# Experts taken in a mixed order of their rank, and one S5 table step issued a unit later

## Chip, core and metric

The kernel runs on one core of a Trainium2 chip, in one launch. The metric is the device time of a run in microseconds (us); lower is better. Its engines have these names here: PE (matrix products), DVE (vector), ACT (scalar and activation), POOL (GpSimd), SP (only issues transfers in this kernel). Each engine works through its own queue in order and waits for others by semaphores.

## What is computed

A two-layer trunk over 256 tokens of width 1024, all in float32. The two places that the change touches are the S5 layer and the expert layer behind it; in front of them stand an attention layer and a dense feed-forward layer (FFN). Cut to what matters:

```python
# S5: 64 groups of 16 channels, each with a 64-dim complex state
y = Re(C x_t),  x_t = a x_{t-1} + B u_t          # a, B, C are complex tables
# experts: top 2 of 8, width 2816
logits = h @ w_router
gates = softmax over the two largest logits, 0 elsewhere     # (256, 8)
for e in range(8):
    out = out + gates[:, e:e+1] * ((silu(h @ w_gate[e]) * (h @ w_up[e])) @ w_down[e])
```

The sum over the experts may be taken in any order. Each expert has 3 x 1024 x 2816 weights, about 34.6 MB, and all eight are read once.

## The kernel before

**Experts.** `route` computes the router's result on the chip, counts the tokens of each expert, and ranks the experts by that count (`rank`, 1 for the largest). A *place* is a position in the order in which the program works through experts. Which expert stands at a place is only known on the chip: `M` is the 8 x 8 matrix that is one where an expert's rank fits a place, and `self.ci` holds the expert's number of each place, from which SP takes the address of its weights (`unit`). What is fixed when the program is built is the capacity of a place, in blocks of 32 tokens: `CAPS = (4, 3, 3, 3, 3, 2, 2, 2)`. A branch (`overflow`) would serve tokens beyond the capacities.

An expert's weights come in 66 *units* of 512 KB (128 rows x 1024 float32): for each of its three column stages 16, 16 and 12 units of gate and up (`gate_up`; the third kind has the name `rest`, line 1698 and 1701, with pieces 128 wide in place of 256), and 8, 8 and 6 units of `w_down` (`down`, line 1729). For every unit PE does four products per block of 32 tokens, so a unit costs PE an amount in proportion to the capacity, and the transfers the same whatever the capacity. The down products of a stage stand behind the gate and up products of the next stage, those of the third stage behind the first stage of the next expert.

The units land in 36 buffers of 512 KB: 4 + 15 named `raw`, 6 `rawh`, 6 `rawi`, 4 `hT_hi`/`hT_lo` and 1 `rawa`. SP issues the next unit as soon as PE has released a buffer, in the order of the program. So PE can be served from a store of some units ahead. No unit can be fetched before `route` has the expert numbers.

Between the units stand, for the next expert, its gather (`gather`, line 1599), and for the present one the transposes of its selection (`back`, line 1619, once per expert and always at the same place among its `rest` units) and for the one before the scatter (line 1657). They are put there by a list that counts units (`run_queue`).

**S5 tables.** While the FFN runs, `s5_tables` builds the tables `G`, `H`, `L`, `E` of the next layer. It is a written-out schedule: `on(u, fn)` records a step at unit u of the FFN, a unit being one tile of FFN weights on PE, and `tick` runs the steps recorded for a unit after its products. For each quarter q of the table, with t0 = 14 + 10 q: `gc(q)` on POOL (24 operations, at t0 - 5), `expand` on ACT and DVE at t0 and t0 + 3 (it copies `gc`'s result to `s5x`), transposes of it on PE (line 1160) one unit after each, and on POOL the chain `hc(q, 0..3)`, 6 operations each (line 1040), whose result is copied to `H` on ACT by `hc_out(q, 0..3)` (lines 1146 and 1147).

`hc(q, t)` reads the result of `hc(q, t - 1)` and writes one of two halves of a buffer, `HC[:, t % 2]`. `hc(q, t)` is recorded at unit t0 + t and `hc_out(q, t)` at t0 + 3 + t; steps of one unit run in the order of their recording. So `hc(q, 2)` is recorded ahead of `hc_out(q, 0)`, which reads the same half: the copy waits for `hc(q, 2)`, and `hc` waits for no copy of its own quarter. Behind `hc(q, 3)` POOL does `gc(q + 1)`, and behind the last quarter the doubling of `E` (`e_double`) and then the norm's small operations (line 393 to 403) that the FFN's end waits for.

ACT and DVE also split each FFN weight tile into two parts ahead of PE (`hl`, lines 206 and 213), in the same queues as the table's copies.

Of the kernel before, what the change touches and what calls it, by code (L numbers as in the profile page):

```python
# [13 lines left out]
OP = mybir.AluOpType  # L14
# [13 lines left out]
C_M1 = C_SEL + 4  # L28
C_LOW = C_M1 + 4
C_CAP = C_LOW + 64  # L30
N_CONST = C_CAP + 8

CAPS = (4, 3, 3, 3, 3, 2, 2, 2)


def make_consts():
    c = np.zeros((128, N_CONST), np.float32)
    p = np.arange(128)
    c[:, C_ID:C_ID + 128] = np.eye(128)
    c[:, C_ONE:C_ONE + 128] = 1.0  # L40
    c[:, C_CAUS:C_CAUS + 128] = np.where(p[None, :] <= p[:, None], 0.0, NEG)
    c[:, C_TRI:C_TRI + 128] = (p[:, None] < p[None, :])
    c[:, C_IOTA:C_IOTA + 128] = p[None, :] + 1
    s = (p % 32)[:, None]
    t = np.arange(32)[None, :]
    for i, l in enumerate(LEVELS):
        if l == 0:
            m = s == t
        else:
            m = (s // (2 * l) == t // (2 * l)) & (s % (2 * l) < l) & (t % (2 * l) >= l)  # L50
        c[:, C_LVL + 32 * i:C_LVL + 32 * i + 32] = m
    for hp in range(4):
        for base in (0, 32):
            c[base + 2 * hp, C_SEL + hp] = 1.0
            c[64 + base + 2 * hp + 1, C_SEL + hp] = 1.0
    m1 = ((p // 32) % 2 == 0)
    c[:, C_M1] = m1
    c[:, C_M1 + 1] = ~m1
    c[:, C_M1 + 2] = -1.0 * ~m1
    c[:, C_CAP:C_CAP + 8] = 32.0 * np.array(CAPS)  # L60
    c[:, C_LOW:C_LOW + 64] = np.tril(np.ones((8, 8)), -1).reshape(64)
    return c

# [187 lines left out]
class Trunk:  # L251
# [10 lines left out]
    def on(self, u, fn):  # L262

        assert u > self.u
        self.sched.setdefault(u, []).append(fn)
# [770 lines left out]
    def s5_tables(self, u0):  # L1036
# [3 lines left out]
        tt = lambda o, x, y, op, e=v: e.tensor_tensor(out=o, in0=x, in1=y, op=op)  # L1040
        ts = lambda o, i, s1, s2, p, q, e=v: e.tensor_scalar(out=o, in0=i, scalar1=s1, scalar2=s2, op0=p, op1=q)
        on = lambda u, fn: self.on(u0 + u, fn)
# [69 lines left out]
        def cmul(o_r, o_i, x_r, x_i, y_r, y_i, tmp):  # L1112

            tt(o_r, x_r, y_r, OP.mult, g)
            tt(tmp, x_i, y_i, OP.mult, g)
            tt(o_r, o_r, tmp, OP.subtract, g)
            tt(o_i, x_r, y_i, OP.mult, g)
            tt(tmp, x_i, y_r, OP.mult, g)
            tt(o_i, o_i, tmp, OP.add, g)
# [3 lines left out]
        def gc(q):  # L1123

            sl = slice(8 * q, 8 * q + 8)
            GC = st["GC"] = kp.tile([128, 2, 8, 4, 16], F32, name="s5gc", tag="gate", bufs=1)
            cmul(GC[:, 0, :, 3], GC[:, 1, :, 3], bc[:, 0, sl], bc[:, 1, sl], cb(fr, sl), cb(fi, sl), tile_t())
            for t in (2, 1, 0):
                cmul(GC[:, 0, :, t], GC[:, 1, :, t], GC[:, 0, :, t + 1], GC[:, 1, :, t + 1], cb(ar, sl), cb(ai, sl),
                     tile_t())  # L1130

        def hc(q, t):

            sl = slice(8 * q, 8 * q + 8)
            if t == 0:
                st["x"] = bc[:, 2, sl], bc[:, 3, sl]
            o_r, o_i = st["HC"][:, t % 2, 0], st["HC"][:, t % 2, 1]
            cmul(o_r, o_i, *st["x"], cb(ar, sl), cb(ai, sl), tile_t())
            st["x"] = o_r, o_i
# [9 lines left out]
        def expand(u):  # L1149
            for i in range(2):  # L1150
                for h in range(2):
                    P = slice(64 * h, 64 * h + 64)
                    (v.tensor_copy if h else a.copy)(
                        st["X"][P, i].rearrange("p r t h k -> p (r t) h k")[:, :, h, :],
                        st["GC"][P, i, 4 * u:4 * u + 4].rearrange("p r t k -> p (r t) k"))

        def g_T(i):
            p = st["gT"] = self.ps([128, 4, 128])
            for r in range(4):
                nc.tensor.transpose(p[:, r, :], st["X"][:, i, r].rearrange("p t h k -> p (t h k)"), self.ident)  # L1160

        def g_out(q, u, i):
            r0 = 8 * q + 4 * u
            (v.tensor_copy if i else a.copy)(self.G[:, r0:r0 + 4, i, :], st["gT"])
# [89 lines left out]
        for q in range(4):  # L1254
            t0 = T0 + PER * q
            if q:
                on(t0 - 5, lambda q=q: gc(q))
            on(t0, lambda: expand(0))
            on(t0 + 1, lambda: g_T(0))
            on(t0 + 2, lambda q=q: (g_out(q, 0, 0), g_T(1), lag(q, 0)))  # L1260
            on(t0 + 3, lambda q=q: (g_out(q, 0, 1), lag_out(), expand(1)))
            on(t0 + 4, lambda q=q: (lag_T(0), g_T(0)))
            on(t0 + 5, lambda q=q: (g_out(q, 1, 0), g_T(1), lag(q, 1)))
            on(t0 + 6, lambda q=q: (g_out(q, 1, 1), lag_out()))
            on(t0 + 7, lambda: lag_T(1))
            on(t0 + 8, lambda q=q: l_out(q))
            for t in range(4):
                on(t0 + t, lambda q=q, t=t: hc(q, t))
                on(t0 + 3 + t, lambda q=q, t=t: hc_out(q, t))
        t0 = T0 + PER * 4 - 1  # L1270
        on(t0, e_begin)
# [183 lines left out]
    def route(self):  # L1455
        nc, kp, ex = self.nc, self.keep, self.ex
        v, a, g = nc.vector, nc.scalar, nc.gpsimd
        tt = lambda o, x, y, op, e=v: e.tensor_tensor(out=o, in0=x, in1=y, op=op)
# [23 lines left out]
        c = kp.tile([128, 2, 8, 16], F32, name="rcmp", tag="t2k", bufs=4)  # L1482
        r = ex.tile([128, 2, 8, 1], F32, name="rrank")
# [7 lines left out]
        r = r.rearrange("p t e o -> p t (e o)")  # L1491
# [19 lines left out]
        c = kp.tile([128, 8, 16], F32, name="rcmp", tag="t2k", bufs=4)  # L1511
# [4 lines left out]
        rank = ex.tile([128, 8], F32, name="rk")  # L1516
        v.tensor_reduce(out=rank, in_=c, axis=AX.X, op=OP.add)
        v.tensor_scalar(out=rank, in0=rank, scalar1=1.0, scalar2=None, op0=OP.add)
        iota = self.cst[:, C_IOTA:C_IOTA + 8]
        mt = kp.tile([128, 5, 8, 8], F32, name="rmt", tag="t2k", bufs=4)  # L1520
        M = ex.tile([128, 8, 8], F32, name="rM")
        tt(M, rank.unsqueeze(1).to_broadcast([128, 8, 8]), iota.unsqueeze(2).to_broadcast([128, 8, 8]), OP.is_equal)
        tt(mt[:, 0], M, iota.unsqueeze(1).to_broadcast([128, 8, 8]), OP.mult)
        pl = ex.tile([128, 8], F32, name="rpl")
        v.tensor_reduce(out=pl, in_=mt[:, 0], axis=AX.X, op=OP.add)
# [66 lines left out]
    def gather(self, e, part):  # L1592

        n = 32 * CAPS[e]
        p = self.gat[part] = self.ps([128, 4, 128])[:, :, :n]
# [6 lines left out]
    def gather_out(self, e, part):  # L1602
# [3 lines left out]
        for j in range(4):  # L1606
            k = 4 * part + j
            o = self.xT[e][:, k, :32 * CAPS[e]]
            if e == 0 and j % 2:
# [28 lines left out]
    def rows_hi(self, e, x):  # L1638

        n = 32 * CAPS[e]  # L1640
        h = self.keep.tile([128, 512], F32R, name="yh", tag="t2k", bufs=4)[:n]
# [3 lines left out]
    def rows_lo(self, e, x):  # L1645
        n = 32 * CAPS[e]
        l = self.keep.tile([128, 512], F32R, name="yl", tag="t2k", bufs=4)[:n]
# [4 lines left out]
    def scatter(self, e, i, p=None):  # L1652
# [3 lines left out]
        for n, y in enumerate(self.yp[x]):  # L1656
            self.nc.tensor.matmul(p, self.B[e][:32 * CAPS[e], t, :], y, start=(n == 0), stop=(n == 1))

# [404 lines left out]
    def setup(self):  # L2063
        nc, I, kp = self.nc, self.ins, self.keep
        self.cst = kp.tile([128, N_CONST], F32, name="cst")
        nc.scalar.dma_start(out=self.cst[:, C_C:C_C + 8], in_=I["consts"][:, C_C:C_C + 8])
# [134 lines left out]
```

## Time and profile before

| | us |
|---|---|
| median of 3 runs | 1375.65 |
| lowest, highest run | 1372.13, 1376.98 |
| the profiled execution's own time | 1371.33 |
| its span, first to last instruction | 1369.6 |
| PE busy | 1234.4 (90% of the span) |
| PE weight loads busy | 991.2 (72%) |
| DVE, ACT, POOL busy | 622.3, 364.7, 269.3 |

The span is divided as the program is: to about 180 us the attention projections, then attention and output projection, the FFN with the S5 tables from about 200 to 456 us, S5 to about 600 us, and from 612 us the experts, more than half of the span. The profiled execution took 1.73 us more than its span. Busy shares are means over stages with different limits.

### The profile page before, as it was taken

The numbers are of one execution on the slowest core, as the hardware profiler recorded it, in microseconds if no ns is written. First come the engines' busy times: TensorE is split into PE (matmuls) and PEld (weight loads), VectorE is DVE, ScalarE is ACT, GpSimd is POOL, SyncE is SP. The second block draws the span as 40 slices with busy tenths as digits, with TensorE's granted clock in tenths as the row PEclk, the third lists the DMA queues.
The fourth block names the chain that finished last, engine by engine and source line by source line (L and its number), as shares of the span: only waits on it lengthen the run. The fifth ranks groups of instructions, "written<-read, shape, count | busy, mean of one in ns | idle before, by whom it ended". The sixth has DMA issues, their size and how long they took to land. (4 is left out here: it accounts for less than half of the span.)

```text
span 1369.6 us, 42688 instructions
## 1 busy us (share of the span) xinstructions
PE 1234.4 (90%) x18635; PEld 991.2 (72%) x18635; DVE 622.3 (45%) x1074; ACT 364.7 (27%) x808; POOL 269.3 (20%) x324
## 2 busy tenths in 40 slices
PE   4998988689997698989989999999999999999885
PEld 4976877679886697886676779976589875756353
DVE  6999898678878686652000310310311202121113
ACT  4455444354553465720000010110010010101001
POOL 1000036999949353000000000000000000000000
PEclk9999999799999898899999999999999999999997
DMA  9867648587887221319999999989989999999994
GB/s 346 273 225 231 213 136 266 168 263 248 271 266 230 77 64 62 109 35 408 407 407 327 380 332 369 406 302 390 400 290 405 386 327 407 407 407 406 408 402 186
DMA packets 138722, 398.57 MB, mean 291 GB/s; under 512 B 12288, under 2 KB 45312, under 8 KB 138400
## 3 DMA queue, kind: packets, MB, share of 16 engines
q1 hardware_dynamic: 138176, 394.62, 79.0%
q8 instruction: 148, 2.42, 0.7%
q0 software_dynamic: 208, 1.15, 0.3%
q14 instruction: 46, 0.38, 0.1%
q10 hardware_dynamic: 144, 0.00, 0.0%
HBM read 394.67 MB, written 1.05 MB: 289 GB/s over the span
## 5 line engine op out<-in xcount | busy, mean ns | idle before, releaser
L1712 DVE TENSOR_TENSOR eh<-gu,eh 128x256 f32<-128x256 f32 (+1 forms) x66 | 25.1, 381 | 433.6 <-ACT eh L1711 433.4
L288 PE MATMUL ps<-hT_hi,hl 128*128 128x256 f32 x576 | 173.4, 301 | 13.6 <-DVE hT_hi L441 5.5
L213 DVE TENSOR_TENSOR hl<-raw,hl 128x1024 fp32r<-128x1024 f32 x121 | 159.2, 1321 | 54.3 <-ACT hl L206 54.0
L1689 PE MATMUL gu<-raw,xTs 128*32 128x256 f32 x3032 | 173.0, 379 | 2.7 <-DMA raw<-in_o_exp_up_dram 1.7
L290 PE MATMUL ps<-hT_hi,hl 128*128 128x256 f32 x576 | 170.2, 295 | 4.6 <-DVE hl L213 4.6
L289 PE MATMUL ps<-hT_lo,hl 128*128 128x256 f32 x576 | 170.4, 296 | 3.0 <-DVE hT_lo L848 2.5
L393 POOL TENSOR_TENSOR ss<-ss 128x1 f32<-128x1 f32 x10 | 2.8, 276 | 845.2 <-ACT ps L386 764.5
L206 ACT ACTIVATE hl<-raw 128x1024 fp32r<-128x1024 f32 x121 | 126.8, 1058 | 156.0 <-DMA raw<-in_e_ffn_up_dram 37.5
L1689 PEld LDWEIGHTS gu<-raw,xTs 128*32 128x32 f32 x3032 | 118.9, 110 | 51.4 <-DMA raw<-in_o_exp_up_dram 6.2
L288 PEld LDWEIGHTS ps<-hT_hi,hl 128*128 128x128 f32 x576 | 117.2, 204 | 16.7 <-DVE hT_hi L441 5.9
L1729 PE MATMUL dn<-raw,eh 128*32 128x256 f32 x2032 | 121.1, 380 | 3.1 <-DMA raw<-in_o_exp_down_dram 1.7
L290 PEld LDWEIGHTS ps<-hT_hi,hl 128*128 128x128 f32 x576 | 116.8, 203 | 6.2 <-DVE hl L213 6.2
L289 PEld LDWEIGHTS ps<-hT_lo,hl 128*128 128x128 f32 x576 | 117.1, 203 | 5.0 <-DVE hT_lo L848 3.4
L1711 ACT ACTIVATE eh<-gu 128x256 f32<-128x256 f32 (+1 forms) x66 | 22.9, 348 | 336.4 <-PE gu L1689 301.0
L1729 PEld LDWEIGHTS dn<-raw,eh 128*32 128x32 f32 x2032 | 77.1, 110 | 40.2 <-DMA raw<-in_o_exp_down_dram 6.1
L1722 DVE STREAM_TRANSPOSE eh<-eh 128x256 f32<-128x256 f32 (+1 forms) x66 | 27.1, 420 | 96.5 <-PE dn L1729 95.8
L1613 ACT ACTIVATE xTs<-ps,colo_mod_ffn,colo_mod_ffn 128x96 f32<-128x96 f32 (+2 forms) x60 | 20.8, 422 | 164.9 <-PE ps L1599 163.9
L1689 PE MATMUL gu<-rawh,xTs 128*32 128x256 f32 x992 | 58.0, 379 | 0.6 <-DMA rawh<-in_o_exp_up_dram 0.6
L1698 PE MATMUL gu<-raw,xTs 128*32 128x128 f32 x1664 | 50.2, 273 | 5.1 <-issue 4.8
L1698 PEld LDWEIGHTS gu<-raw,xTs 128*32 128x32 f32 x1664 | 45.3, 110 | 7.9 <-issue 5.6
L1689 PEld LDWEIGHTS gu<-rawh,xTs 128*32 128x32 f32 x992 | 37.3, 110 | 18.3 <-DMA rawh<-in_o_exp_up_dram 2.1
L1689 PE MATMUL gu<-rawi,xTs 128*32 128x256 f32 x848 | 49.4, 379 | 0.0
(418 smaller groups left out, 2182.5 us busy)
## 6 DMA issues: line engine op xcount, KB each, us to landing
raw<-in_o_exp_down_dram SPq DMA_DIRECT2D x92, 512.0 KB, 10.0
raw<-in_o_exp_gate_dram SPq DMA_DIRECT2D x68, 512.0 KB, 6.9
raw<-in_o_exp_up_dram SPq DMA_DIRECT2D x67, 512.0 KB, 6.6
raw<-in_o_exp_rest_dram SPq DMA_DIRECT2D x58, 512.0 KB, 10.1
rawi<-in_o_exp_down_dram SPq DMA_DIRECT2D x30, 512.0 KB, 6.7
rawh<-in_o_exp_down_dram SPq DMA_DIRECT2D x27, 512.0 KB, 6.4
raw<-in_e_mod_ffn_w_dram SPq DMA_DIRECT2D x24, 512.0 KB, 4.5
raw<-in_o_mod_mix_w_dram SPq DMA_DIRECT2D x24, 512.0 KB, 4.6
```

Source lines behind the costliest of these rows:

```text
L206: nc.scalar.activation(hi, raw, AF.Copy)
L213: nc.vector.tensor_tensor(out=lo, in0=raw, in1=hi.bitcast(F32), op=OP.subtract)
L288: mm(out, lh, rh, start=start, stop=False)
L289: mm(out, lh, rl, start=False, stop=False)
L290: mm(out, ll, rh, start=False, stop=stop)
L1613: nc.scalar.activation(o, p[:, j, :], AF.Identity, bias=sh[:, k:k + 1], scale=A[:, k:k + 1])
L1689: mm(gu[i][cg(j), o:o + 256], xT[:, k, cg(i)], raw[:, 256 * j:256 * j + 256], start=(o == 0 and k == 0), stop=(o > 0 and k == NCH - 1))
L1698: mm(gu[i][cg(j), 128 * h:128 * h + 128], xT[:, u, cg(i)], w, start=(u == h == 0), stop=False)
L1711: nc.scalar.activation(eh[:, i, 0:w], gu[i][:, 0:w], AF.Silu)
L1712: nc.vector.tensor_tensor(out=eh[:, i, 0:w], in0=gu[i][:, w:2 * w], in1=eh[:, i, 0:w], op=OP.mult)
L1722: nc.vector.transpose(hT[:, i, 0:w], eh[:, i, 0:w])
L1729: mm(dn[i // 2][cg(j), 256 * (i % 2):256 * (i % 2) + 256], hT[:, i, c:c + 32], raw[:, 256 * j:256 * j + 256], start=(b == f == i % 2 == 0) ...
```

## The change

The order of the ranks at the places becomes 0 1 5 2 3 6 4 7. The table `RANKS` sets it, the capacities of the places follow it (4, 3, 2, 3, 3, 2, 3, 2), and `M` compares each expert's rank with a row of constants in place of 1 to 8. The constants grow by 8 columns. In the S5 tables `hc(q, t)` is recorded one unit later, at t0 + 1 + t.

```diff
-N_CONST = C_CAP + 8
-
-CAPS = (4, 3, 3, 3, 3, 2, 2, 2)
+C_ORD = C_CAP + 8
+N_CONST = C_ORD + 8
+
+RANKS = (0, 1, 5, 2, 3, 6, 4, 7)
+CAPS = tuple((4, 3, 3, 3, 3, 2, 2, 2)[r] for r in RANKS)
...
+    c[:, C_ORD:C_ORD + 8] = 1.0 + np.array(RANKS)
...
-                on(t0 + t, lambda q=q, t=t: hc(q, t))
+                on(t0 + 1 + t, lambda q=q, t=t: hc(q, t))
...
-        tt(M, rank.unsqueeze(1).to_broadcast([128, 8, 8]), iota.unsqueeze(2).to_broadcast([128, 8, 8]), OP.is_equal)
+        tt(M, rank.unsqueeze(1).to_broadcast([128, 8, 8]),
+           self.cst[:, C_ORD:C_ORD + 8].unsqueeze(2).to_broadcast([128, 8, 8]), OP.is_equal)
```

The lines behind the first hunk stand 3 or 4 lower in the changed file. Three places show how the instructions move.

First, PE at the seventh place, from `back` to the first down units of the expert. `gu_6280` to `gu_6282` are the accumulators of its blocks of 32 tokens for gate and up, `dn_6284` and `dn_6285` those of the down product (two blocks each). Before:

```order
L1619 MATMUL ps_13834<-cst,P 128x128 x2
L1621 MATMUL ps_13834<-rgp,P 128x1 x2
L1701 MATMUL gu_6280<-raw_13355,xTs 32x128 x8
L1701 MATMUL gu_6281<-raw_13355,xTs 32x128 x8
...
L1729 MATMUL dn_6284<-raw_13411,eh 32x256 x8
L1729 MATMUL dn_6284<-raw_13421,eh 32x256 x8
```

And now:

```order
L1623 MATMUL ps_13745<-cst,P 128x128 x2
L1625 MATMUL ps_13745<-rgp,P 128x1 x2
L1705 MATMUL gu_6280<-raw_13094,xTs 32x128 x8
L1705 MATMUL gu_6281<-raw_13094,xTs 32x128 x8
L1705 MATMUL gu_6282<-raw_13094,xTs 32x128 x8
...
L1733 MATMUL dn_6284<-raw_13163,eh 32x256 x8
L1733 MATMUL dn_6285<-raw_13163,eh 32x256 x4
```

The seventh place now has three blocks of tokens per unit in place of two; the third place has two in place of three, and the others keep theirs. The number of products over all places is the same.

Second, DVE from the seventh place to the eighth: the products of gate and up (`eh`, one row for each block), the transposes of them, and the rows of the expert that has just ended (`y`). Before, both places have two blocks and the rows of the seventh are taken in one group of 8 (line 1635); now they stand thus:

```order
L1726 STREAM_TRANSPOSE eh<-eh 128x192 x3
L1716 TENSOR_TENSOR eh<-gu_6280,eh 128x256
L1716 TENSOR_TENSOR eh<-gu_6281,eh 128x256
L1726 STREAM_TRANSPOSE eh<-eh 128x256 x2
L1639 TENSOR_TENSOR y<-dn_6284,gate 32x256 x8
L1639 TENSOR_TENSOR y<-dn_6285,gate 32x256 x4
L1652 SCALAR_TENSOR_TENSOR yl<-y,wslot,yh 96x512 x2
```

An expert of three blocks is now followed by one of two at three places (before at one), and the rows of the larger one are done among the units of the smaller one.

Third, POOL in the first quarter of the S5 tables, with what each row waits for: the last operation of `hc(0, 1)` (its first five stand ahead of it) and the six of `hc(0, 2)`. `Pool_49` is POOL's own earlier result, `Activation_49` one of ACT. Before:

```order
L1040 TENSOR_TENSOR s5m_2014<-s5m_2014 128x128 [waits Pool_49]
L1040 TENSOR_TENSOR s5m_2014<-s5m_2014,s5k_2010 128x128
L1040 TENSOR_TENSOR s5m_2014<-s5m_2014,s5k_2010 128x128 [waits Pool_49]
L1040 TENSOR_TENSOR s5m_2014<-s5m_2014 128x128 [waits Pool_49]
L1040 TENSOR_TENSOR s5m_2014<-s5m_2014,s5k_2010 128x128
L1040 TENSOR_TENSOR s5m_2014<-s5m_2014,s5k_2010 128x128 [waits Pool_49]
L1040 TENSOR_TENSOR s5m_2014<-s5m_2014 128x128 [waits Pool_49]
```

And now:

```order
L1043 TENSOR_TENSOR s5m_2014<-s5m_2014 128x128 [waits Pool_49]
L1043 TENSOR_TENSOR s5m_2014<-s5m_2014,s5k_2010 128x128 [waits Activation_49]
L1043 TENSOR_TENSOR s5m_2014<-s5m_2014,s5k_2010 128x128 [waits Pool_49]
L1043 TENSOR_TENSOR s5m_2014<-s5m_2014 128x128 [waits Pool_49]
L1043 TENSOR_TENSOR s5m_2014<-s5m_2014,s5k_2010 128x128 [waits Activation_49]
L1043 TENSOR_TENSOR s5m_2014<-s5m_2014,s5k_2010 128x128 [waits Pool_49]
L1043 TENSOR_TENSOR s5m_2014<-s5m_2014 128x128 [waits Pool_49]
```

No instruction of POOL has changed its place in POOL's queue, nor one of ACT in ACT's. What has changed are the waits: the first and fourth operation of `hc(q, 2)`, and of `hc(q, 3)`, now wait for the copies `hc_out(q, 0)` and `hc_out(q, 1)` on ACT, and those copies wait for `hc(q, 0)` and `hc(q, 1)` in place of `hc(q, 2)` and `hc(q, 3)`.

## Rows read from the trace of the kernel before

**Rows 1.** The page's slices: bandwidth in GB/s, in 40 slices of 34.2 us.

```profile
GB/s 346 273 225 231 213 136 266 168 263 248 271 266 230 77 64 62 109 35 408 407 407 327 380 332 369 406 302 390 400 290 405 386 327 407 407 407 406 408 402 186
```

**Rows 2.** Windows: length, busy us of PE to POOL, PEclk, DMA share, GB/s.

```profile
996.00:1011.00 15.00, 15.00 (x428) 14.24 (x424) 1.41 (x5) 2.80 (x8) 0.00 (x0) 1.00 0.85 280
1170.00:1181.00 11.00, 11.00 (x292) 10.47 (x287) 0.83 (x4) 2.59 (x8) 0.00 (x0) 1.00 1.03 406
1272.00:1310.00 38.00, 30.61 (x454) 12.22 (x450) 7.29 (x16) 2.98 (x6) 0.00 (x0) 1.00 1.03 408
```

**Rows 3.** Timeline of PE: start, us, operation, count, [idle before]; 16 units of capacity two.

```profile
1124.08 12.46 PE L1689 MATMUL gu<-raw,xTs 128*32 128x256 f32 x224
1136.16 2.10 PE L1689 MATMUL gu<-hT_hi,xTs 128*32 128x256 f32 x32
```

**Rows 4.** Timeline of PE: `back` of the fourth to eighth place.

```profile
1012.69 0.44 PE L1619 MATMUL ps<-cst,P 128*128 128x128 f32 x2
...
1108.50 0.44 PE L1619 MATMUL ps<-cst,P 128*128 128x128 f32 x2
...
1181.88 0.44 PE L1619 MATMUL ps<-cst,P 128*128 128x128 f32 x2
...
1249.54 0.44 PE L1619 MATMUL ps<-cst,P 128*128 128x128 f32 x2
...
1330.08 0.44 PE L1619 MATMUL ps<-cst,P 128*128 128x128 f32 x2
```

**Rows 5.** Timeline of PE: first unit waited for, and the last down unit.

```profile
1272.41 1.07 PE L1689 MATMUL gu<-rawa,xTs 128*32 128x256 f32 x16 [0.19 <-DMA rawa<-in_o_exp_up_dram]
...
1350.46 1.07 PE L1729 MATMUL dn<-rawh,eh 128*32 128x256 f32 x16
```

**Rows 6.** PE's groups of lines, sixth `back` to seventh: busy us, mean ns.

```profile
L1599 PE MATMUL ps<-P,xn 128*128 128x64 f32 x32 | 4.0, 278 | 0.0
```

**Rows 7.** Waits of PE, first place (611 to 739 us): us, times, longest.

```profile
PE gu L1698 <- issue: 4.0, 3, 2.5
...
PE ps L1619 <- issue: 2.2, 1, 2.2
PE gu L1701 <- issue: 2.0, 1, 2.0
```

**Rows 8.** Waits of PE, second to fifth place (739 to 1124 us).

```profile
PE gu L1701 <- issue: 4.6, 5, 1.7
```

**Rows 9.** Waits of PE, sixth and seventh place (1124 to 1262 us).

```profile
PE gu L1701 <- issue: 1.9, 2, 1.0
PE dn L1729 <- issue: 1.6, 2, 1.0
```

**Rows 10.** Timeline of POOL: `hc(2, 2)`, `gc(3)` and `hc(3, 0)` from their first, and `E`.

```profile
323.92 1.74 POOL L1040 TENSOR_TENSOR s5m<-s5m,s5k 128x128 f32<-128x128 f32 x2
...
337.60 0.90 POOL L1040 TENSOR_TENSOR s5gc<-s5bc,s5k 128x128 f32<-128x128 f32 x1 [2.35 <-DVE s5x L1153]
...
357.70 2.73 POOL L1040 TENSOR_TENSOR s5m<-s5bc,s5k 128x128 f32<-128x128 f32 x2
...
397.26 0.27 POOL L1212 COPY E<-s5c 128x32 f32<-128x32 f32 x1 [14.87 <-DVE s5c L1040]
```

**Rows 11.** Timeline of ACT: a copy of `hc_out(0, 1)`, one of `hc_out(2, 0)`, `expand` of quarter 3.

```profile
261.58 0.31 ACT L1147 ACTIVATE H<-s5m 64x128 f32<-64x128 f32 x1 [2.23 <-POOL s5m L1040]
...
336.08 0.29 ACT L1146 COPY H<-s5m 64x128 f32<-64x128 f32 x1
...
359.26 0.70 ACT L1153 COPY s5x<-s5gc 64x256 f32<-64x256 f32 x2
```

**Rows 12.** Timeline of PE: table transposes of quarters 0 and 3, and the FFN's end.

```profile
263.08 1.12 PE L1160 MATMUL ps<-cst,s5x 128*128 128x128 f32 x4 [3.31 <-ACT fsil L962]
...
362.13 0.63 PE L1160 MATMUL ps<-cst,s5x 128*128 128x128 f32 x4 [0.42 <-DVE s5x L1153]
...
456.80 3.45 PE L418 MATMUL ps<-rd,X 128*128 128x128 f32 x15 [10.13 <-POOL rd L403]
```

## Prediction

> **What bounds the kernel now.** I read the bandwidth slices first. From slice 19 on, where the experts begin, they stand at 407 or 408 GB/s except at some dips (302, 290) and, near the end, five slices in a row at 406 to 408 [rows 1]. So the experts, more than half of the span, have two regimes, and I took a window of each. Among the `rest` units of the fourth place PE is busy for all of its 15.00 us while the DMA share is 0.85: PE sets the pace, the buffers are full and SP waits for them. Among those of the sixth place the share is 1.03, but PE still fills its 11.00 us: it eats from the store. In the eighth place PE is busy for 30.61 of 38.00 us with the share again at 1.03: the store is empty and the transfers set the pace [rows 2]. PEclk is 1.00 in all three, so no part of this is the clock.
>
> Two rates give the store's account. At capacity two, 14 units (224 records, 16 for a unit) stand on PE from 1124.08 to 1136.16, 0.863 us for a unit [rows 3], so 1.295 at capacity three and 1.73 at four. At 408 GB/s [rows 2] a unit of 524,288 bytes lands every 1.285 us. With the other products of a place the distance between two `back`s is the time of a place: 95.8 us from the fourth to the fifth (capacity three), 67.66 from the sixth to the seventh (capacity two), and 80.54 from the seventh to the eighth, which also has capacity two [rows 4]. In 95.8 us 74.6 units can land and 66 are used: the store gains 8.6. In 67.66 us 52.7 land: it loses 13.3. PE first waits for a unit at 1272.41 [rows 5], 22.9 us behind the seventh `back`: less 2.5 for other products and gaps that is 24 units, 11 of the seventh place and some 12 of the eighth, which cost the store 4 more. Two places of capacity two have taken 26.6 units and a little was left for the third. A full store is thus some 27 to 31 of the 36 buffers (I go on with 27), and three small places in a row are one too many.
>
> **The order of the ranks.** Capacities become 4 3 2 3 3 2 3 2. PE's products are as many as before. Full at the end of the second place, the store goes 27, 14, 22, 27 (31, but it can't hold more), 14, 22, and 9 after the last place: it never empties, and PE sets the pace to its last unit. What that is worth is what the eighth place loses now. Between the last two `back`s PE would need the 67.66 us of the place before, less one gather (4.0 us [rows 6]), since `gather` is that of the next expert and behind the seventh `back` none is left: 63.7 in place of 80.54, a gain of 16.9. Behind the last `back`, at 1330.08, PE has 17 units left, 3 `rest` and 14 of `down`, and ends them at 1350.46 + 1.07 = 1351.53 [rows 5], after 21.45 us. At its own pace they take 17 x 0.863 = 14.7, plus 0.7 for the transposes of `back`, plus 1.75 for gaps as in the sixth and seventh place (1.9 + 1.6 over two places [rows 9]): 17.1, a gain of 4.3. Together **-21.2**. The chain behind the last unit, down to the output, keeps its length, since the last place has two blocks before and after.
>
> **What the same order may give back.** PE's waits in the experts that no semaphore explains ("issue") stand almost all at `rest` lines 1698 and 1701, where the pieces are half as wide and PE asks for twice the instructions per microsecond. At the first place, capacity four, they come to 4.0 + 2.2 + 2.0 = 8.2 us [rows 7]; at the four places of capacity three to 4.6, or 1.15 each [rows 8]; at the sixth and seventh to 1.9, or 0.95 each [rows 9]. The larger sum goes with transfers that fill the engines: the middle places have a DMA share of 0.85 among these units, the sixth 1.03 [rows 2]. What no row shows is a place of capacity three with the share at 1.03. The new order makes two such (fourth and seventh, both refilling the store) and perhaps a third (the fifth). By the nearest rows it costs between 1.15, nothing new, and the 8.2 of capacity four. Capacity three lies midway between the two saturated cases, (8.2 + 0.95) / 2 = 4.6, so I take 3.4 more at two places: **+6.9**, with bounds 0 and 3 x 7.05 = 21.2.
>
> The Trainium skill would put this term near nothing: "Runtime: NRT & Kernel Launch", section "Instruction fetch mechanics", says that the sequencer fetches the next block of instructions through a DMA queue of its own while it executes the present one, and that the cost of crossing a block is mostly hidden. By that the sum would be the first rival's below. The 8.2 us of the first place speak against it [rows 7].
>
> The comparison for `M` reads a row of constants in place of a counter; it has the same shape, and I take it at nothing, as I do the 8 more columns of constants among the weights that load at the start.
>
> **The S5 tables.** No instruction moves on POOL or ACT; the waits turn round. Before, ACT's copy of `hc_out(0, 1)` stood 2.23 us for POOL's `hc(0, 3)` [rows 11], and PE's table transposes at 263.08 came 3.31 us late behind ACT's `fsil` [rows 12]. The copy now needs only `hc(0, 1)`: I take 2.0 of it as gained, 2.2 at most. The price is that `hc(q, 2)` now waits for a copy that stands in ACT's queue behind the weight splits. It is largest in the third quarter: `hc(2, 2)` started at 323.92 [rows 10], and the copy it now needs, `hc_out(2, 0)`, ran at 336.08 + 0.29 [rows 11], 12.45 us later. Behind it POOL still has `hc(2, 2)` and `hc(2, 3)`, 11.3 us (323.92 to the wait before 337.60, that is 335.25), then `gc(3)`, 20.1 us (337.60 to 357.70) [rows 10]: 336.37 + 11.3 + 20.1 = 367.8. ACT asked for that result at 359.26 [rows 11], and PE's transposes of it ran at 362.13 [rows 12]. With some 0.8 for the copies they would now run at 368.6, 6.5 us late. What covers it is the weight tiles that ACT and DVE have already split ahead of PE; if that cover is several tiles PE loses nothing, if none 6.5. No row shows how far it reaches, so I take the middle, 3.3. Later POOL has 14.87 us of idle time before `E` [rows 10] that absorbs one such delay. A second one of the same size, in the last quarter, would leave (12.45 - 2.35) + 12.45 - 14.87 = 7.7 for the end of the FFN, where PE already waits 10.13 us for POOL [rows 12]; one or the other ends last there, not both. Net 3.3 - 2.0 = **+1.3**, bounds -2.2 and +7.7.
>
> **Sum.** -21.2 + 6.9 + 1.3 = -13.0 on the profiled execution's own 1371.33: 1358.3. That execution lies 2.7 below the mean of the four that are known (1374.0), so a run should give **1361.0**. A difference of 0.3%, 4.1 us, is about what a measurement of this kernel can tell from none; faster thus means below 1370, slower above 1378.
>
> **Rivals.**
> First, the issue gaps don't grow. For it: at the sixth and seventh place they stay at 0.95 with the share at 1.03. Against it: the first place. -21.2 + 1.3 = -19.9, a run of 1354.1; with the S5 part at its best 1350.6. Chance 0.27.
> Second, the other side: the gaps at the three places of capacity three that may be saturated are four each, as in the first two rows of waits at the first place together, and each as long as the longest there, 2.5 us [rows 7]. That is 10 us a place, 8.85 more than now: +26.6 - 21.2 + 1.3 = +6.7, a run of 1380.7. It decides from 1.15 + 19.9 / 3 = 7.8 us a place on. Capacity three asks for no more instructions per microsecond than capacity two, which speaks against it. Chance 0.06.
> Third, the S5 tables pay in full: -21.2 + 6.9 + 7.7 = -6.6, a run of 1367.4. For it: POOL's queue is long and in order, and DVE and ACT take the table's copies and the weight splits in one queue, so a late table holds up the splits too. Chance 0.16.
> Fourth, the order doesn't do what the account says: the store doesn't refill at 8.6 units a place, because buffers are released in another rhythm, and PE waits as long as now, only elsewhere. Against it: 390 to 407 GB/s in the slices after the first place [rows 1]. A run of about 1374. Chance 0.05.
> The forecast itself has 0.46.
>
> **Range and chances.** 1352 to 1371 holds the forecast, nearly all of the first rival and of the third with its bound, and leaves out the second, the fourth and the edges, less than 2 in 10. Faster: 0.46 + 0.27 + half of the third, 0.81. Slower: the second and a little of the fourth, 0.07. The rest, 0.12, within 0.3%.
>
> **What would show it.** Right: no wait of PE for a transfer in the last place, `back`s 67 to 68 us apart after small places and 96 to 101 after those of capacity three, the last unit at about 1338, and the last weights issued well ahead of it. The issue waits at lines 1698 and 1701 (now 1702 and 1705) some 4.6 us at the fourth and the seventh place, with a DMA share of 1.03 there. POOL waiting for ACT at `hc`, 12 us in the third quarter, and PE or ACT waiting for `s5gc` some microseconds near 360 us. Wrong: PE still waiting for weights in the last places, issue waits of 8 us and more at each place of capacity three, or an FFN that ends more than 5 us later than before; and in the other direction, gaps that stay at 1 us.

## The result and the profile after

The changed kernel took 1363.25 us (median of 7 runs, 1360.06 to 1370.51) against 1373.78 (7 runs, 1367.21 to 1376.98): 10.5 us less, a ratio of 0.993 with a 95% interval of 0.9911 to 0.9949. The prediction was 1361.0, range 1352 to 1371. The profiled execution has a span of 1358.3 us, 11.3 below that of before. Divided at PE's instructions:

| stretch | before | after | |
|---|---|---|---|
| start to the norm ahead of the FFN | 174.22 | 175.22 | +1.00 |
| FFN with the S5 tables, to PE's first product of the next norm | 282.58 | 276.63 | -5.95 |
| S5 and the router, to the first gather | 155.14 | 155.21 | +0.07 |
| experts, first gather to the end of the last down unit | 739.59 | 733.03 | -6.56 |
| tail | 18.07 | 18.21 | +0.14 |

So the total was as forecast, and its parts were not: the forecast had -14.3 in the experts (-21.2 + 6.9) and +1.3 in the FFN.

The page's bandwidth line, beside [rows 1]:

```profile
GB/s 344 279 225 230 212 121 264 233 233 282 257 259 223 78 66 60 110 34 408 407 407 328 383 335 355 407 407 407 407 403 402 349 381 407 406 408 406 401 375 37
```

The transfers now run at over 400 GB/s from slice 26 on with one dip (349, 381), and end before the program does (375, 37). Windows, with the columns of [rows 2]: `rest` units of the fourth and of the fifth place, and a stretch of the eighth:

```profile
970.00:981.00 11.00, 8.46 (x241) 7.63 (x231) 0.00 (x0) 2.33 (x7) 0.00 (x0) 1.00 1.03 407
1068.00:1081.00 13.00, 12.46 (x326) 11.53 (x320) 0.00 (x0) 2.59 (x8) 0.00 (x0) 1.00 0.85 297
1270.00:1310.00 40.00, 40.00 (x706) 23.17 (x698) 11.07 (x23) 2.99 (x6) 0.00 (x0) 1.00 1.02 406
```

The eighth place, which had PE busy for 30.61 of 38.00 us, now has it busy for all of 40.00: the store holds. The fourth place, of capacity three, has a share of 1.03 as forecast, and PE is idle there for 2.54 of 11.00 us. In the fifth the share is 0.85, the buffers are full, and 0.54 of 13.00 us is idle. PEclk is 1.00 throughout. PE's waits from 600 us to the end, in us, times, longest:

```profile
PE gu L1702 <- issue: 11.5, 9, 2.5
PE gu L1705 <- issue: 11.2, 9, 2.0
PE dn L1733 <- issue: 4.6, 5, 1.4
PE ps L1603 <- DVE P L1592: 3.5, 1, 3.5
PE gu L1661 <- ACT yh L1647: 3.5, 1, 3.5
PE ps L1623 <- issue: 2.2, 1, 2.2
PE ps L1603 <- issue: 0.2, 1, 0.2
```

No wait for a transfer is left, where the last place had 7.9 us of them, the two largest groups being

```profile
PE dn L1729 <- DMA rawh<-in_o_exp_down_dram: 1.8, 1, 1.8
PE gu L1689 <- DMA raw<-in_o_exp_up_dram: 1.7, 8, 0.3
```

The "issue" waits come to 29.7 us; by the same view of before they were 19.2. The `back`s, in the timeline of PE:

```profile
816.63 0.44 PE L1623 MATMUL ps<-cst,P 128*128 128x128 f32 x2
890.49 0.44 PE L1623 MATMUL ps<-cst,P 128*128 128x128 f32 x2
982.99 0.44 PE L1623 MATMUL ps<-cst,P 128*128 128x128 f32 x2
1081.30 0.44 PE L1623 MATMUL ps<-cst,P 128*128 128x128 f32 x2
1155.22 0.44 PE L1623 MATMUL ps<-cst,P 128*128 128x128 f32 x2
1248.06 0.44 PE L1623 MATMUL ps<-cst,P 128*128 128x128 f32 x2
1322.38 0.44 PE L1623 MATMUL ps<-cst,P 128*128 128x128 f32 x2
```

Behind a `back` 17 units still run at the old capacity and 49 at the new one before the next. Taking that work off the distances (at 0.863 us a unit of capacity two and 1.295 of three) leaves what a place costs beyond its units. The third to fifth place, all of capacity three, had 10.0 to 10.5 before; now the fourth has 92.50 - 78.1 = 14.4, the fifth 12.8, the seventh 14.7. The last place, which had 23.6, has 10.0.

### The profile page after: what moved, and what is told of

It is laid out like the page before. It is cut to its first block, busy times and chain, and to the rows that moved or that the text cites. A ratio compares the mean times of both kernels' runs of the same rounds, so it can differ in the third digit from the quotient of the medians.

```text
span 1358.3 us, 42680 instructions
## 1 busy us (share of the span) xinstructions
PE 1221.1 (90%) x18635; PEld 960.5 (71%) x18635; DVE 617.1 (45%) x1074; ACT 364.8 (27%) x808; POOL 270.0 (20%) x324
## 5 line engine op out<-in xcount | busy, mean ns | idle before, releaser
L1693 PEld LDWEIGHTS gu<-raw,xTs 128*32 128x32 f32 x3016 | 107.0, 110 | 58.0
L291 PEld LDWEIGHTS ps<-hT_hi,hl 128*128 128x128 f32 x576 | 115.5, 200 | 16.0 <-DVE hT_hi L444 5.9
L293 PEld LDWEIGHTS ps<-hT_hi,hl 128*128 128x128 f32 x576 | 114.8, 199 | 7.4 <-DVE hl L216 7.4
L1726 DVE STREAM_TRANSPOSE eh<-eh 128x256 f32<-128x256 f32 (+1 forms) x66 | 26.9, 419 | 96.7 <-PE dn L1733 96.0
L1702 PE MATMUL gu<-raw,xTs 128*32 128x128 f32 x1792 | 54.3, 273 | 8.6 <-issue 8.6
L1702 PEld LDWEIGHTS gu<-raw,xTs 128*32 128x32 f32 x1792 | 49.3, 110 | 11.6 <-issue 10.2
```

The costliest lines, as they stand in the source:

```text
L291: mm(out, lh, rh, start=start, stop=False)
L293: mm(out, ll, rh, start=False, stop=stop)
L1693: mm(gu[i][cg(j), o:o + 256], xT[:, k, cg(i)], raw[:, 256 * j:256 * j + 256], start=(o == 0 and k == 0), stop=(o > 0 and k == NCH - 1))
L1702: mm(gu[i][cg(j), 128 * h:128 * h + 128], xT[:, u, cg(i)], w, start=(u == h == 0), stop=False)
L1726: nc.vector.transpose(hT[:, i, 0:w], eh[:, i, 0:w])
```

## The experiments

Every kernel below differs from the changed one by the edit shown; ratios are to the kernel before, with a 95% interval. "Experts" and "FFN" are the stretches of the table above in the one execution that was profiled.

| kernel | ratio (interval) | experts | issue waits there | FFN |
|---|---|---|---|---|
| ranks_only | 0.9962 (0.9943 to 0.9981) | 733.48 | 29.7 | 282.95 |
| s5_only | 0.9971 (0.9953 to 0.9989) | 739.27 | 18.8 | 280.10 |
| small_mid | 1.0047 (1.0025 to 1.0068) | 745.83 | 26.3 | 278.47 |
| quarter_units | 1324.41 us, one run | 694.79 | 0.0 | 278.10 |
| h_early | 0.9966 (0.9949 to 0.9982) | 733.18 | 29.8 | 279.80 |
| h_early_step_early | 0.9956 (0.9937 to 0.9974) | 733.17 | 25.9 | 281.93 |
| rest_wide | 0.9728 (0.9706 to 0.9749) | 704.41 | 5.4 | 281.62 |
| order_b | 0.9929 (0.9908 to 0.9949) | 733.50 | 28.6 | 281.18 |
| wide_desc | 0.991 (0.9887 to 0.9934) | 727.94 | 4.4 | 275.53 |
| wide_order_b | 0.9787 (0.9754 to 0.9821) | 711.06 | 4.5 | 279.59 |
| wide_step_early | 0.9764 (0.974 to 0.9789) | 706.69 | 6.4 | 282.00 |
| wide_step_0_3 | 0.9736 (0.9705 to 0.9767) | 704.14 | 5.5 | 282.35 |

**Each half of the change alone.** ranks_only puts the S5 step back:

```diff
-                on(t0 + 1 + t, lambda q=q, t=t: hc(q, t))
+                on(t0 + t, lambda q=q, t=t: hc(q, t))
```

> The new order of the ranks with the S5 step where it was before. Theory: the order is worth 6 to 7 us in the expert layer (first gather to last down unit 733 us in place of 739.6), and the FFN ends as before (PE resumes for the norm near 456.8): 0.995 of before. Rival: the order brings the whole 11 us, because the FFN part of the changed kernel only happened to be shorter in the one execution that was profiled: 0.992. The profile tells by DVE's copy of the first quarter's s5x, 7.1 us before and 2.3 for two with the change.

s5_only puts the ranks back (`RANKS = (0, 1, 2, 3, 4, 5, 6, 7)`).

> The S5 step one unit later, with the ranks descending as before. Theory: 4 to 6 us of gain, all before the FFN's end (PE resumes for the norm near 452), none in the expert layer: 0.996 of before. Rival 1: the step itself is worth nothing or loses 1 to 7 us as its price in the third quarter said, and the shorter FFN came from where DVE's copy happened to fall against POOL's memset of H: 1.000 to 1.005. POOL's waits at hc for ACT should show 1 to 3 us, not 12, in either case.

0.9962 and 0.9971: the halves add up (0.9962 x 0.9971 = 0.9933), and neither rival holds. The order gives 6 us in the experts, the same to within half a microsecond in every narrow kernel that has it or order_b. The step gives some 4 us by these times, which the forecast had as a loss; PE resumed for the norm at 457.14 us in the profile of s5_only, not near 452: its FFN began at 177.04 and took 280.10.

**Is it three small places in a row, wherever they stand?** small_mid, `RANKS = (0, 1, 5, 6, 7, 2, 3, 4)`:

> The changed kernel with the capacities 4 3 2 2 2 3 3 3 (order 0 1 5 6 7 2 3 4): three small places in a row in the middle. Theory (a store of some 27 units, emptied by three small places wherever they stand): PE waits for transfers in the fifth place, 13 to 20 us lost there, and the three places of capacity three behind it refill the store with the transfers at a share of 1.03 and so have issue waits of 4 to 6 us each; 10 to 25 us slower than the changed kernel, 0.999 to 1.01 of before. Rival (what costs is that the small places end the program, since nothing behind them hides the transfers): no wait for transfers that lasts, as fast as the changed kernel or faster, 0.99 of before.

The theory held. The experts took 12.8 us longer than with the mixed order, and PE's waits there show transfers again, the largest group being

```profile
PE gu L1693 <- DMA raw<-in_o_exp_up_dram: 2.5, 12, 0.2
```

with 9.1 us over all groups. They stand in the fifth place, as expected: it cost 25.5 us beyond its units and the small place before it 10.4. Standing at the end of the program is not what made the last place slow.

**Where the issue waits come from.** quarter_units fetches a quarter of each expert unit; three quarters of the weights are left out of the result:

```diff
-                b.nc.sync.dma_start(out=t, in_=src())
+                b.nc.sync.dma_start(out=t[:, 0:256], in_=src()[:, 0:256])
...
-                        mm(gu[i][cg(j), o:o + 256], xT[:, k, cg(i)], raw[:, 256 * j:256 * j + 256],
+                        mm(gu[i][cg(j), o:o + 256], xT[:, k, cg(i)], raw[:, 0:256],
```

(the `rest` and `down` products alike).

> The changed kernel with only the first 256 columns of each expert unit fetched, a quarter of the bytes, and PE's products reading those columns in place of the others, with the same number and shape of products: the expert layer without the load of the transfers. Theory (issue waits come from instructions that are fetched over the same DMA engines): the issue waits at the rest lines fall from 22.7 us in all to under 5, those of the first place too, and the expert layer is 15 to 20 us shorter. Rival (PE's sequencer itself can't supply products of half the width at this rate, more so at capacity four): the waits stay at 15 us or more.

The issue waits vanished, in the first place too, and the experts were 38.2 us shorter with every product still there: twice what was expected. (A `rest` unit takes eight products of 128 columns for each block of 32 tokens, where a gate or up unit takes four of 256. The trace has two records for each product; "recorded products" counts these.) A window in the `rest` units of the fourth place, columns as in [rows 2]:

```profile
960.00:975.00 15.00, 15.00 (x425) 13.41 (x418) 1.43 (x6) 3.12 (x12) 0.00 (x0) 1.00 0.30 86
```

425 recorded products in 15.00 us, none waited for, at a DMA share of 0.30. So PE's sequencer can supply them, and it is the load of the transfers that makes it wait. The page's DMA part for the changed kernel has the instructions as a queue of their own on the same engines:

```profile
q1 hardware_dynamic: 138176, 394.62, 78.5%
q8 instruction: 148, 2.42, 0.7%
```

The times of these 148 packets, of 16,384 bytes each, show the cause directly. Each of the 25 issue waits in the changed kernel's experts ended 1.31 to 1.60 us after one of them had landed, and each of the 17 of before 1.26 to 1.62 us after. It is so for all 201 issue waits in the experts of the thirteen kernels that have any (1.21 to 1.63 us). Waits that follow each other stand 128 recorded products apart, and their packets mostly 6.2 us apart. In quarter_units the same 25 products started at least 1.8 us after their packet had landed. A packet itself lasted no longer under load (1.07 us on the mean in the experts, 1.08 in quarter_units); it came later.

The numbers also say which stretches wait. On the `rest` lines of quarter_units the recorded products stand 26.9 ns apart on the mean, on the wide gate and up line 53.5. By these, 128 narrow products last 3.4 us, less than the 6.2 between packets, and 128 wide ones 6.8, more than that (an estimate from the two means). And the 38.2 us are the same waits: product by product, 36.1 of them stand at the starts of those 25. The list of waits gives 29.7 because it counts only from the end of the product before, which the profile models.

The other test is fewer instructions. rest_wide takes the first eight `rest` units of a stage, whose two halves share their weights, in one product of 256 columns in place of two of 128:

```diff
+                if u < 8:
+                    w2 = raw.rearrange("p (h j c) -> p h j c", h=2, j=4)
+                    for j in range(4):
+                        mm(gu[i][cg(j), 0:256].rearrange("p (h c) -> p h c", h=2), xT[:, u, cg(i)], w2[:, :, j, :],
+                           start=(u == 0), stop=False)
+                    return
```

> The changed kernel with the first eight of the twelve rest units of each stage in products 256 columns wide (two runs of 128 in one instruction) in place of two of 128: the same columns, half the instructions there. Theory (PE's issue waits are instructions that arrive late over the loaded DMA engines): the issue waits at these units fall from 11.5 us to under 4, those at the last four units (11.2) by some as well since less is due, and the expert layer is 6 to 14 us shorter: 0.983 to 0.989 of before. Rival (the waits come at fixed places or from the transfers of weights, not from the number of instructions): waits and time as in the changed kernel, 0.993.

The experts took 28.6 us less than the changed kernel's, more than expected, at an unchanged DMA share of 1.03 in the `rest` units of the fourth place:

```profile
960.00:975.00 15.00, 15.00 (x254) 10.67 (x248) 0.00 (x0) 2.79 (x8) 0.00 (x0) 1.00 1.03 407
```

PE's issue waits in the experts:

```profile
PE dn L1735 <- issue: 3.5, 4, 1.1
...
PE gu L1707 <- issue: 1.9, 2, 1.1
```

The waits at the eight wide units are gone, and those at the four narrow ones behind them (line 1707, unchanged code) fell from 11.2 to 1.9. The rival is out. At 1337.84 us (1334.27 to 1338.27) this kernel beats both others.

**What the order is worth without the issue waits.** wide_desc is rest_wide with the ranks descending:

> The kernel with the wide rest products, with the ranks descending (capacities 4 3 3 3 3 2 2 2). Theory (the order takes 19 to 21 us of waiting for transfers off the last place and gives 14 back as issue waits): with wide products there are no issue waits to give back, so the order is worth its full 17 to 22 us here. The first five places lose their issue waits (13 us of 739.5), the last place waits for transfers as before: expert layer about 725 us in place of 704.4 with the mixed order, 0.985 to 0.990 of before. Rival (the order is worth about 6 us whatever PE's products look like): expert layer about 711 us, 0.978 of before.

727.94 against 704.41: the order is worth 23.5 us here, a little over the 17 to 22 expected, and 5.8 to 6.6 with narrow products. The theory held, and this is the cleanest evidence for the two opposite terms.

**Other orders.** order_b, `RANKS = (0, 1, 2, 5, 3, 6, 4, 7)`:

> The changed kernel with the small places at 4, 6 and 8 (order 0 1 2 5 3 6 4 7, capacities 4 3 3 2 3 2 3 2). Theory: the store goes 27, 14, 22, 9, 17, 4 and stays above nothing; the place of capacity three behind another, which in the changed kernel still took 2.5 us more than with a full store, is now served from a full store, so 1 to 3 us faster than the changed kernel, 0.991 to 0.993 of before. Rival (the store is smaller than 27, or the last place starves): PE waits for transfers in the last place and the kernel is 3 us or more slower than the changed one, 0.995 or more.

Neither: nothing starved, and nothing was gained. Its third place, served from a full store, cost 9.2 us beyond its units in place of 12.8 for the changed kernel's fifth; but its sixth, a small place with the transfers at full rate ahead of it and in it, cost 11.9 in place of 9.6. Issue waits go with the time at full rate, not only with capacity three.

wide_order_b is the same order with wide products.

> The kernel with the wide rest products and capacities 4 3 3 2 3 2 3 2. Theory: with no issue waits the places of capacity three cost the same wherever they stand, and the store stays above nothing by some 4 units, a little less than before since PE is faster: within 2 us of the mixed order, 0.972 to 0.975 of before. Rival: the store runs dry in the last place, 3 us or more slower, with waits for transfers of down units.

Here the rival holds: the experts took 711.06 us, with 3.9 us of waits for transfers in the last place. Faster products empty the store sooner, and the spare 4 units of the account were not there.

**Why the step gains.** My first explanation was a copy on DVE that stands while POOL clears `H`. The rows of before, DVE and then POOL:

```profile
236.45 7.10 DVE L1153 COPY s5x<-s5gc 64x256 f32<-64x256 f32 x1 [0.82 <-POOL s5gc L1040]
...
236.35 7.05 POOL L1241 MEMSET H<- 128x2048 f32 x4
```

The copy of 0.38 us lasts as long as the four memsets. h_early clears `H` ahead of `gc(0)`:

```diff
-        on(9, lambda: (alloc_G(), gc(0), c_expand()))
-        on(10, lambda: alloc_H())
+        on(9, lambda: (alloc_G(), alloc_H(), gc(0), c_expand()))
```

> The changed kernel with POOL's clearing of H (four memsets, 7.3 us) moved ahead of gc(0), into POOL's idle time of 30 us before it. Theory A (the S5 step's gain is an accident of where the clearing falls: DVE's copy of s5x stood for 7.1 us in both kernels with the step early, 2.3 to 5.8 us with it late, and PE waited and then ran at the lower clock): the copies take under 1 us in all, the FFN ends 2 to 5 us earlier than in the changed kernel, 0.990 of before, and the kernel with the step early and the same move is as fast. Theory B (the gain is ACT's waits for POOL at the copies to H): no more than 2 us against the changed kernel.

> The same, with the S5 step where it was before the change (new order of ranks, clearing of H moved). Theory A: as fast as the kernel with the step late and the clearing moved, 0.990 of before. Theory B: 4 us slower than that one, near 0.994, with ACT waiting 4 to 8 us for POOL at the copies to H.

The copies fell to 0.38 and 0.48 us, and neither kernel became faster (0.9966 and 0.9956). The DVE timeline of h_early shows where the 7 us went:

```profile
180.80 13.45 DVE L444 CAST hT_hi<-hf 128x256 fp32r<-128x256 f32 x1
```

A cast that takes 0.29 us elsewhere stands from 180.80 to 194.25, as long as POOL clears `Cx`, `s5x`, `L` and now `H` in a row (180.95 to 194.10; in the changed kernel the same cast lasts 6.47 us). The stall was moved, not removed, so this pair can't decide between A and B. Theory A's gain did not appear, and neither did the 4 us that theory B expected between the two: the kernel with the step late is only 0.7 us faster by the medians, and by the ratios, whose intervals overlap, it is no faster. h_early is some 5 us slower than the changed kernel (0.9966 against 0.993); why, no run here shows. (order_b has the late step and a copy of 7.10 us.)

What decided was to lay all profiles side by side at PE's table transposes. From the third group of the first quarter to the fourth, the four kernels with the step early took 6.8, 6.0, 5.5 and 7.8 us and all nine with it late 3.2 to 3.3. The rows of ranks_only (early):

```profile
259.46 0.63 PE L1163 MATMUL ps<-cst,s5x 128*128 128x128 f32 x4 [0.34 <-DVE s5x L1156]
265.44 0.66 PE L1163 MATMUL ps<-cst,s5x 128*128 128x128 f32 x4 [2.50 <-ACT fsil L965]
```

what ACT did ahead of that `fsil`:

```profile
259.20 0.30 ACT L1149 COPY H<-s5m 64x128 f32<-64x128 f32 x1 [1.33 <-POOL s5m L1043]
261.42 0.31 ACT L1150 ACTIVATE H<-s5m 64x128 f32<-64x128 f32 x1 [1.93 <-POOL s5m L1043]
```

and PE in the changed kernel:

```profile
251.58 0.63 PE L1163 MATMUL ps<-cst,s5x 128*128 128x128 f32 x4 [1.80 <-ACT fhh L977]
254.86 0.60 PE L1163 MATMUL ps<-cst,s5x 128*128 128x128 f32 x4
```

The price is as visible. From the third group of the third quarter to the second of the fourth, the early kernels took 27.6 us on the mean and the nine late ones 30.4. The cause is `gc(3)` on POOL: behind that third group it started 8.1 to 8.6 us later in eight of the late kernels and 6.8 in quarter_units, and within 0.2 us of it in the early ones. ACT in the changed kernel, at `expand` of the last quarter:

```profile
356.54 0.40 ACT L1156 COPY s5x<-s5gc 64x256 f32<-64x256 f32 x1 [4.15 <-POOL s5gc L1043]
357.84 0.41 ACT L1156 COPY s5x<-s5gc 64x256 f32<-64x256 f32 x1 [0.90 <-POOL s5gc L1043]
```

Two more kernels tested this with wide products. wide_step_early, with the diff of ranks_only:

> The kernel with the wide rest products, with the S5 step where it was before the change: a third pair for the step alone. Theory (the step is worth 3 to 4 us in the FFN, as in the two pairs that are run): 3 to 4 us slower than the wide kernel, 0.975 to 0.976 of before, FFN of 282 to 283 us in its profile. Rival (the step is worth nothing, and the pairs differed by chance, as the pair with H cleared earlier showed no difference): 0.972 to 0.974, within 1.5 us of it.

wide_step_0_3, `on(t0 + (q in (0, 3)) + t, ...)` (its "sixth group" is the third of that quarter):

> The kernel with the wide rest products, with the S5 step one unit later in the first and last quarter only, where the thirteen profiles so far show the gain, and at its old place in the second and third, where POOL's wait at hc(2, 2) holds up gc(3). From the sixth transpose group of the third quarter to the second of the fourth, PE took 27.6 us with the step early (four profiles) and 30.4 with it late (nine). Theory (gain and price are at those places and separate): third to fourth transpose group of the first quarter 3.3 us as with the step late (6.5 early); the stretch into the fourth quarter back at 27 to 28 us; FFN of 275 to 278 us (279.0 late, 282.4 early); 0.970 to 0.973 of before. Rival (gc(3) is late for another reason, or the gain in the first quarter needs the later quarters): the stretch stays at 30 us, FFN 279 us or more.

The first came out as the theory said by its time, 0.9764 against 0.9728, though the two intervals just touch. Its profile doesn't confirm the place: its FFN of 282.00 us is only 0.4 above the 281.62 of rest_wide, and 2.3 us of the difference stands in the experts. So three of the four pairs that differ in the step alone give it some 4 to 5 us, and the pair with `H` cleared early none. The second was no faster than rest_wide (0.9736), and its theory held half: 3.3 us in the first quarter, and 26.95 in the stretch into the fourth, but the next stretch, between the last two groups of the table, took 5.34 us as with the step early (5.1 on the mean, 3.4 late) in spite of the late step there, and the FFN 282.35 where 275 to 278 was expected. POOL, which came to the last quarter earlier, then waited 3.22 and 1.65 us for ACT. `gc(3)` started 0.5 us behind the third group, as with the step early. Gain and price are at those two places, but they are not separate.

## Why the forecast was right, and where its terms were not

- **The store and the starved last place (-21.2).** Right in mechanism: small_mid, wide_desc and the last place's 40.00 of 40.00 us show it. In size: behind the last `back` 21.45 us became 17.71, -3.7 for the forecast -4.3; with wide products, which empty the store sooner, the order is worth 23.5. The spacing that I gave as a sign, 67 to 68 us after small places, was wrong: the 17 units behind a `back` at the old capacity make it 73.9 there, and 92.5 for a place of three after a small one. The sums don't change by it. The store's size holds too, if the buffers are taken as full at the `back` of 1108.50: the unit that PE first waited for, at 1272.41, was the 155th from there (22 behind the seventh `back`, not 24, were used before it), and 127.6 could land meanwhile, which leaves 27.4.
- **The issue waits given back (+6.9).** The step that failed in size: "I take 3.4 more at two places". The two places measured 4.2 and 4.5 beyond the 10.2 of before. But the fifth place cost 2.6 more, since the `rest` units behind its predecessor's `back` belong to it, and the last 3.3 more than a small place without a gather (10.7 - 4.0): 14.6 together, which is 21.2 - 6.6. What the forecast lacked was the time between packets of instructions beside the time that PE needs for one (6.2 and 3.4 us). The rule that I weighed there (the Trainium skill, "Runtime: NRT & Kernel Launch", section "Instruction fetch mechanics": the cost of crossing a block of instructions is mostly hidden) holds in quarter_units, with 0.0 us of waits at a share of 0.30, and fails at full transfer rate, with 29.7. The Trainium skill, "DMA: Bandwidth & Descriptors", section "Queues, rings and completion order", says that a DMA engine takes turns between its queues by whole packets; that the waits go with the load of the weights' queue agrees.
- **The S5 step (+1.3).** The place of the gain and of the price were right, and the price too: 3.3 forecast, 2.8 measured (30.4 - 27.6). The gain was under-sized. "I take 2.0 of it as gained" counted one of ACT's waits; PE gained 3.2 between the third and fourth group and 1.7 at the same place of the last quarter, by means 2.3 more between the second and third, where early (7.3 to 12.6 us) and late kernels (7.0 to 11.7) overlap. With some 1.0 lost elsewhere the FFN was 279.0 us on the mean of the nine late profiles, 282.4 on that of the four early ones: -3.4. POOL's wait at `hc(2, 2)` was 1.98 us in the changed kernel, up to 7.4 in others, and never the 12.45 that I read from the copy's place in the trace of before; ACT runs earlier there when it no longer waits in the first quarter. That the price still came near 3.3 is in part luck: I took the middle of a range whose cover no row showed.
- **The rest of the FFN's -5.95** is this execution's own: the FFN's length varies by 6 us over the late profiles. One part that varies is DVE's copy against the clearing of `H`: 2.33 us for two copies here, 4.41 to 7.82 in most others. TensorE's granted clock varies with it. PE in the kernel before, then the window of 240 to 260 us before and after:

```profile
243.70 1.09 PE L1160 MATMUL ps<-cst,s5x 128*128 128x128 f32 x4 [4.45 <-DVE s5x L1153]
...
240.00:260.00 20.00, 13.72 (x97) 12.60 (x97) 15.68 (x13) 5.99 (x13) 19.45 (x25) 0.74 0.54 175
240.00:260.00 20.00, 13.22 (x154) 11.69 (x154) 13.57 (x14) 11.30 (x26) 19.38 (x27) 1.00 0.75 236
```

  Before, the granted clock fell to the lower of its two levels (1.2 and 2.4 GHz) during PE's wait for that copy and stood there from 241.5 to 251.8 us; after, it was at the upper one throughout the window. Of the whole FFN the two shortest (276.63 and 275.53 us, with copies of 2.3 us) have 31 and 30 us at the lower level, the other seven late ones 41 to 46 and the early ones 47 to 54. That the clock makes the FFN longer, and does not only follow PE's waits, isn't shown.
- The total came out because two terms were off in opposite directions, 7.7 us more given back and 4.7 more gained in the FFN than forecast (by the means), not because each was right.

That POOL ends the FFN was right: from its first copy of `E` to its `rd` it took 58.3 to 59.2 us in all fourteen profiles (early, late and mixed), so the FFN ends when `E` could start.

## What to carry to other kernels

When weights stream at full rate, count instructions as well as bytes: 64 products of 128 columns replaced by 32 of 256, for each stage and block of tokens, were worth some 26 us, two and a half times the change that was studied. A packet of instructions should keep PE busy for longer than the next one takes to come, 6.2 us here. An order of work that removes a starved stretch keeps the transfers at full rate for longer, and what goes over the same engines, PE's instructions here, then pays; look for such waits in a stretch that is already saturated before summing. And one profile of a stretch that varies by 6 us can't price a 3 us edit: milestones within the stretch, over several kernels that share it, can.

## What was not expected of the hardware

A short DVE instruction stood for as long as POOL cleared memory, through several memsets in a row: 7.10 us beside 7.05 (four memsets), 6.47 beside 6.2 (three), 13.45 beside 13.15 (seven). The Trainium skill, "SBUF — State Buffer", section "SBUF: two separate sides", says that GpSimd and a DVE instruction in a two-port mode share a port pair as an exclusive lock, held for a whole instruction by whichever starts first. The traces agree that DVE is shut out, and here it was so over up to seven instructions of POOL, not one; that these copies and casts run in that mode, no run here shows. It is not always so: in the changed kernel two copies took 2.33 us while the clearing of `H` went on for 7.37.

Instructions came to PE over the same DMA engines as the weights, in packets of 16,384 bytes. With those engines at a share of 1.03 they came some 6.2 us apart in the `rest` units, too slowly for 128 narrow products (3.4 us), and PE started again 1.2 to 1.6 us after the landing that it waited for.
